# A gate table built from bf16 one-hot rows and three bf16 weight pieces, two tokens at a time

## The chip, the cores and the metric

The kernel runs on one core of a Trainium2 chip. TensorE (PE in the profile) multiplies matrices, and its weight loads have a row of their own (PEld). VectorE (DVE), ScalarE (ACT) and GpSimd (POOL) work on elements, SyncE (SP) issues DMAs. Every number is in microseconds (us) of device time unless it is marked ns, and the metric is the time of one launch.

## The reference, cut to what matters

The reference is one encoder block: two attention branches, an output projection, then a PEER layer with 16,384 experts and a final norm. The change lies in the PEER layer alone:

```python
def block(xb):                       # 128 tokens
    q = (xb @ w_q).reshape(PEER_BLOCK, PEER_HEADS, 2, PEER_HALF)
    ...
    idx = jnp.take_along_axis(cand_i, top_pos, axis=-1)      # i1*128 + i2
    g = jax.nn.softmax(top_s, axis=-1).reshape(PEER_BLOCK, -1)
    h = jnp.einsum('tkd,td->tk', u[idx], xb)
    act = g * jax.nn.gelu(h, approximate=False)
    return jnp.einsum('tk,tkd->td', act, v[idx])
```

Each token uses 8 heads x 16 = 128 experts. An expert has two keys, `i1` and `i2`, each below 128, and a gate weight `g`.

## The kernel before, in words

Everything is in fp32 precision: a matrix product is three fp32r matmuls (helper `mm3`, lines 218 to 221), of a high and a low half of each operand. The halves of a weight tile are made by `wtile`: DMA by SP (L206), high half by ACT (L207), low half by DVE (L208).

Of the 512 tokens, the first 352 (`ND`) are *dense*: the kernel computes all 16,384 experts for them and multiplies each by a gate that is zero where the token did not choose the expert. The other 160 tokens are served by gathered rows (L1115, by POOL; used by DVE at L1126 and L1133). The dense part has two long loops:

- the loop over `e` at L1171 (called the first expert loop here): 128 steps, each of two half steps with 24 matmuls of 128x352; ACT applies gelu (L1192) and stores the result to memory;
- the loop over `i` at L1242 (the second expert loop), which loads gelu results and gates, multiplies them and multiplies by `v`.

The gates come from a table built during the first loop. The generator `gates_of` (L1005) makes it for each of three token tiles (128, 128 and 96 tokens). The keys and gate weights are turned so that the 128 choices of a token lie on the partitions. For one token, the table of 128x128 gates is the product of two one-hot matrices: `oh1[k, i2]` as TensorE's moving or stationary side, and `oh0[k, i1]` scaled by the gate weight. Four tokens go together: DVE compares both keys with 0..127 (L1025, one instruction for 8 rows of 128), ACT scales `oh0` by the high and by the low half of the weight (L1022, eight instructions), and TensorE runs eight fp32r matmuls of 128x128 (L1033), two to each token. `gate_out` (L1040) has ACT copy the bank of four tokens from PSUM (L1053, two instructions), and POOL sends 32 tokens at a time to memory (L1058). One `next(gate_steps)` in each half step (L1186) moves this on; a bank of four tokens takes two half steps. The one-hot rows and their scaled copies lie in unused columns of `hgh` and `hgl` (`spare`, L999).

`routing` (L1063) runs in the same loop, ahead of the gates: the top 16 of the candidates of each token tile, on DVE (L842 to L888). The order of each engine's instructions is made by the framework's scheduler from the order in which the program emits them.

Of the kernel before, what the change touches and what calls it, by code (L numbers as in the profile page):

```python
# [9 lines left out]
F32 = mybir.dt.float32  # L10
F32R = mybir.dt.float32r
BF16 = mybir.dt.bfloat16
# [38 lines left out]
CONST = {}  # L51


def _constants():
# [16 lines left out]
    out, o = [], 0  # L71
    for k, v in cols.items():
        v = np.asarray(v, np.float64).astype(np.float32)
        CONST[k] = (o, o + v.shape[1])
        o += v.shape[1]
        out.append(v)
    return np.ascontiguousarray(np.concatenate(out, axis=1))
# [30 lines left out]
def _layout(x, positions, meta_tokens, norm_mix_g, w_in, mla_q_norm_g, mla_w_uq, mla_kv_norm_g,  # L108
# [50 lines left out]
    for i, n in enumerate(FRONT):  # L159
# [9 lines left out]
            "pos": c(pos[None]), "gains": c(gains), "const": CONST_ARR,  # L169
# [13 lines left out]
def body(tc, nc, a, dbg=None):  # L183
# [55 lines left out]
    cst = cp.tile([P, CONST_ARR.shape[1]], F32, name="cst")  # L239

    def C(k):
        return cst[:, CONST[k][0]:CONST[k][1]]

# [30 lines left out]
    mp = mixer.enter_context(tc.tile_pool(name="mixer", bufs=1, side="left"))  # L274
    tri_r = mp.tile([P, P], F32R, name="tri_r")
# [64 lines left out]
    SP.dma_start(cst, a["const"])  # L340
# [436 lines left out]
    rh_ = hgp.tile([P, SEQ], F32, name="rh_")  # L777
    rcol = hgp.tile([P, 1], F32, name="rcol")
    rcolb = hgp.tile([P, 1], F32, name="rcolb")

    with tc.tile_pool(name="outp", bufs=2, side="right") as op:
# [8 lines left out]
        for m in range(KC):  # L790
# [23 lines left out]
            gr = (op if m < KC - 1 else hgp).tile([P, 2, P], F32, name="gr")  # L814
# [179 lines left out]
    iota_n = up.tile([P, P], F32, name="iota_n", bufs=1)  # L994
    SP.dma_start(iota_n, a["iota"])
    iota_b = iota_n[:, None, None, :].to_broadcast([P, 2, 4, P])
    gb = {}

    spare = [t[:, :, ND:ND + P].rearrange("p (i c t) k -> p i c t k", i=2, c=2) for t in (hgh, hgl)]  # L999
# [5 lines left out]
    def gates_of(ti):  # L1005
        ef, idx = keys[ti], up.tile([P, 2, P], F32, name="idx", bufs=1)
        wt = up.tile([P, 2, P], F32R, name="wt", bufs=1)
# [4 lines left out]
        S.activation(idx, ps[:, :2 * P].rearrange("p (c t) -> p c t", c=2), AF.Copy)  # L1012
# [306 lines left out]
```

## Time and profile before

| | |
|---|---|
| median of three runs | 3683.48 us (3680.32 to 3684.66) |
| the profiled execution | 3683.72 us |
| its span, first to last instruction | 3681.5 us |
| PE busy, share of the span | 3630.1 us, 99% |
| DVE busy | 2623.8 us, 71% |
| ACT busy | 1475.3 us, 40% |
| matmuls of the gate table (L1033) | 704, from 1689.6 to 2509.2 us |

In the rows below a group of instructions is one line of the kernel on one engine, `out<-in` by tile name, `xN` the count, then the busy time, the mean of one in ns, and the idle time ahead of it with what ended it. Matmuls are pipelined, and the end of one is modelled by the profiler; the distance from start to start tells what one costs. The clock column is the granted clock of TensorE as a share of its full 2.4 GHz.

### The profile page before, as it was taken

To read this page: it belongs to the slowest core of one execution; us is meant where nothing else is said; L and a number is where in the kernel's file an instruction comes from. 1 tells how busy PE (TensorE), PEld (TensorE's weight loads), DVE (VectorE), ACT (ScalarE), POOL (GpSimd) and SP (SyncE) were. 2 spreads that over 40 slices of the span, in tenths; PEclk is the share of its full clock that TensorE was granted. 3 is DMA by queue.
4 is the path that set the end of the run, shared out by engine and by line. 5 is a ranking of instruction groups with operands and counts; after the bars stand their busy time and mean duration, and the time that the engine had idled before them with its cause. 6 is when DMAs were issued, how large, how long until landed. Compare 5 with 4: busy or idle time off the path is not lost. (4 is left out here: it accounts for less than half of the span.)

```text
span 3681.5 us, 53353 instructions
## 1 busy us (share of the span) xinstructions
PE 3630.1 (99%) x21159; PEld 3377.5 (92%) x21159; DVE 2623.8 (71%) x3499; ACT 1475.3 (40%) x2360; POOL 702.1 (19%) x499
## 2 busy tenths in 40 slices
PE   9999999999999999999999999999999999999997
PEld 8888888887788878899999999999999999999997
DVE  5533334335644567899979877777689999999896
ACT  4233233234533232235656666664333333333333
POOL 1000000000011221112222322332232322322220
PEclk9999999999999999999999999999999999999998
DMA  4322222221144442268898989999899999999982
GB/s 167 101 100 92 98 93 97 95 98 41 46 143 138 144 156 87 97 250 298 318 351 309 374 335 341 348 342 362 318 374 368 366 365 365 370 357 348 350 335 96
DMA packets 216538, 868.28 MB, mean 236 GB/s; under 512 B 24352, under 2 KB 49632, under 8 KB 175328
## 3 DMA queue, kind: packets, MB, share of 16 engines
q1 hardware_dynamic: 132896, 463.49, 35.4%
q0 software_dynamic: 53440, 361.52, 25.7%
q10 hardware_dynamic: 29952, 39.86, 3.0%
q8 instruction: 166, 2.72, 0.3%
q14 instruction: 84, 0.69, 0.1%
HBM read 801.83 MB, written 62.95 MB: 235 GB/s over the span
## 5 line engine op out<-in xcount | busy, mean ns | idle before, releaser
L207 ACT ACTIVATE wh<-wr 128x1024 fp32r<-128x1024 f32 (+1 forms) x756 | 789.1, 1054 | 1511.5 <-PE ps L221 1346.2
L208 DVE TENSOR_TENSOR wl<-wr,wh 128x1024 fp32r<-128x1024 f32 (+1 forms) x741 | 935.3, 1270 | 512.4 <-ACT wh L207 507.7
L219 PE MATMUL ps<-hgh,wl 128*128 128x352 f32 (+1 forms) x2304 | 773.2, 336 | 10.5 <-DVE wl L208 9.6
L221 PE MATMUL ps<-hgh,wh 128*128 128x352 f32 (+1 forms) x2304 | 768.3, 333 | 0.0
L220 PE MATMUL ps<-hgl,wh 128*128 128x352 f32 (+1 forms) x2304 | 765.1, 332 | 2.1 <-DVE hgl L225 2.0
L219 PE MATMUL ps<-vah,wl 128*128 128x352 f32 x2048 | 664.0, 324 | 4.1 <-DVE wl L208 3.9
L221 PE MATMUL ps<-vah,wh 128*128 128x352 f32 x2048 | 664.8, 325 | 0.0
L220 PE MATMUL ps<-val,wh 128*128 128x352 f32 x2048 | 661.0, 323 | 0.0
L219 PE MATMUL ps<-xh,wl 128*128 128x512 f32 (+1 forms) x1376 | 472.0, 343 | 6.0 <-ACT xh L312 6.0
L220 PE MATMUL ps<-xl,wh 128*128 128x512 f32 (+1 forms) x1376 | 470.1, 342 | 0.2 <-DVE xl L313 0.2
L221 PE MATMUL ps<-xh,wh 128*128 128x512 f32 (+1 forms) x1376 | 470.1, 342 | 0.0
L219 PEld LDWEIGHTS ps<-hgh,wl 128*128 128x128 f32 x2304 | 434.6, 189 | 25.0 <-DVE wl L208 11.9
L220 PEld LDWEIGHTS ps<-hgl,wh 128*128 128x128 f32 x2304 | 434.3, 189 | 14.5 <-DVE hgl L225 2.8
L221 PEld LDWEIGHTS ps<-hgh,wh 128*128 128x128 f32 x2304 | 433.5, 188 | 11.5 <-issue 0.2
L219 PEld LDWEIGHTS ps<-vah,wl 128*128 128x128 f32 x2048 | 386.2, 189 | 5.2 <-DVE wl L208 5.2
L221 PEld LDWEIGHTS ps<-vah,wh 128*128 128x128 f32 x2048 | 388.5, 190 | 0.0
L220 PEld LDWEIGHTS ps<-val,wh 128*128 128x128 f32 x2048 | 388.3, 190 | 0.0
L1115 POOL DMA_INDIRECT row<-v,eo x128 | 217.4, 1698 | 568.4 <-DVE xg L1133 522.7
L1133 DVE SCALAR_TENSOR_TENSOR xg<-row,act,xg 128x2048 f32<-128x2048 f32 x127 | 298.3, 2349 | 7.8 <-DMA row<-v,eo 7.8
L1115 POOL DMA_INDIRECT row<-u,eo x128 | 186.0, 1453 | 610.7 <-DVE row L1126 537.3
L219 PEld LDWEIGHTS ps<-xh,wl 128*128 128x128 f32 x1376 | 259.5, 189 | 37.8 <-ACT xh L312 6.4
L1126 DVE SCALAR_TENSOR_TENSOR row<-row,xg 128x2048 f32<-128x2048 f32 x128 | 292.5, 2285 | 0.5 <-DMA row<-u,eo 0.5
(453 smaller groups left out, 4744.8 us busy)
## 6 DMA issues: line engine op xcount, KB each, us to landing
wr<-ut SPq DMA_DIRECT2D x256, 512.0 KB, 6.3
wr<-vb SPq DMA_DIRECT2D x256, 512.0 KB, 6.7
wr<-front SPq DMA_DIRECT2D x238, 512.0 KB, 3.3
h_d<-hb ACTq DMA_DIRECT2D x128, 176.0 KB, 5.4
g_d<-gb POOLq DMA_DIRECT2D x44, 512.0 KB, 10.5
gin<-g_d SPq DMA_DIRECT2D x32, 704.0 KB, 5.8
hin<-h_d SPq DMA_DIRECT2D x32, 704.0 KB, 7.9
gates<-gt ACTq DMA_DIRECT2D x32, 256.0 KB, 2.0
```

The costliest lines, as they stand in the source:

```text
L207: more["last"] = S.activation(hi[:, s], raw[:, s], AF.Copy)
L208: more["lo"] = (eng or V).tensor_sub(lo[:, s], raw[:, s], hi[:, s].bitcast(F32))
L219: T.matmul(ps, wl, xh, start=start, stop=False)
L220: T.matmul(ps, wh, xl, start=False, stop=False)
L221: T.matmul(ps, wh, xh, start=False, stop=stop)
L1115: G.indirect_dma_start(out=row[:], out_offset=None, in_=a[src], in_offset=bass.IndirectOffsetOnAxis(ap=idx, axis=0))
L1126: ins = V.scalar_tensor_tensor(row, row, 1.0, xg if k < P else xgb, ALU.mult, ALU.mult, accum_out=act[:, k:k + 1] if k < P else actb[:, k ...
L1133: ins = V.scalar_tensor_tensor(y, row, w, y, ALU.mult, ALU.add)
```

## The change

The table is made from bf16 operands. A one-hot row is exact in bf16. The fp32 gate weight is cut into three bf16 pieces (L1029 to L1034 of the changed kernel), which sum to it exactly: DVE makes them by rounding, subtracting, rounding again and subtracting again. A token's table is now three bf16 matmuls, for the three pieces, into the same PSUM columns.

Two tokens go together, and one step of the generator (a half step of the loop) handles one pair: DVE compares the keys of the pair with 0..127 (one instruction, 512 elements of bf16) and multiplies `oh0` by the smallest piece (one instruction, 256 elements); ACT makes the other two scaled copies (four instructions); TensorE runs six matmuls. The two tokens are interleaved in the innermost dimension, so that DVE's operands are contiguous pairs, while TensorE and ACT read every other element. A bank still holds four tokens. There are three buffers of one-hot rows: two in `rh_`, one new tile. `spare` is not used any more. To make room, the constant table is cut in two, one half of which (`MIXER_CONST`) goes when the attention part ends; the 0..127 row is brought into a buffer of the weight ring and turned to bf16 by ACT into `gr_last`.

```diff
-    SP.dma_start(cst, a["const"])
+    SP.dma_start(csts[0], a["const"])
+    SP.dma_start(csts[1], a["const_m"])
...
-    iota_n = up.tile([P, P], F32, name="iota_n", bufs=1)
-    SP.dma_start(iota_n, a["iota"])
-    iota_b = iota_n[:, None, None, :].to_broadcast([P, 2, 4, P])
...
-    spare = [t[:, :, ND:ND + P].rearrange("p (i c t) k -> p i c t k", i=2, c=2) for t in (hgh, hgl)]
+    iota_f = wp.tile([P, 1024], F32, name="wr", tag="wr", bufs=4)[:, :P]
+    SP.dma_start(iota_f, a["iota"])
+    iota_b = gr_last[:, 0].bitcast(BF16).rearrange("p (k t) -> p k t", t=2)
+    S.activation(iota_b, iota_f[:, :, None].to_broadcast([P, P, 2]), AF.Copy)
+    keys_b = gr_last[:, 1].bitcast(BF16).rearrange("p (c t) -> p c t", c=2)
+    more_oh = up.tile([P, 2, P, 2], BF16, name="more_oh", bufs=1)
+    ohs = list(rh_.bitcast(BF16).rearrange("p (i c k t) -> p i c k t", i=2, c=2, t=2)[:, i] for i in range(2)) + [more_oh]
...
-        split(wt[:, 0], wt[:, 1], ps[:, 2 * P:3 * P])
+        w, rest = ps[:, 2 * P:3 * P], ps[:, 3 * P:]
+        V.tensor_copy(last_b, w)
+        V.tensor_copy(wt[:, 0], last_b)
+        V.tensor_sub(rest, w, wt[:, 0])
+        V.tensor_copy(last_b, rest)
+        V.tensor_copy(wt[:, 1], last_b)
+        V.tensor_sub(last_b, rest, wt[:, 1])
         yield
         n = min(P, ND - ti * P)
-        for t0 in range(0, n + 4, 4):
-            if t0:
-                p0 = t0 - 4
-                oh_, wo_ = (spare[c][:, p0 // 4 % 2] for c in range(2))
-                for t in range(4):
-                    for c in range(2):
-                        after_gelu(S.activation(wo_[:, c, t], oh_[:, 0, t].bitcast(F32), AF.Copy,
-                                                scale=wt[:, c, p0 + t:p0 + t + 1].bitcast(F32)))
-            if t0 < n:
-                V.tensor_tensor(spare[0][:, t0 // 4 % 2], idx[:, :, t0:t0 + 4, None].to_broadcast([P, 2, 4, P]),
-                                iota_b, ALU.is_equal)
+        bank = None
+        for p in range(n // 2 + 2):
+            t0 = 2 * p
+            if 0 < p <= n // 2:
+                for t in range(2):
+                    for c in range(2):
+                        after_gelu(S.activation(wos[:, (p - 1) % 2, c, :, t], ohs[(p - 1) % 3][:, 0, :, t], AF.Copy,
+                                                scale=wt[:, c, t0 - 2 + t:t0 - 1 + t]))
+            if p < n // 2:
+                V.tensor_tensor(ohs[p % 3], keys_b[:, :, None, t0:t0 + 2].to_broadcast([P, 2, P, 2]),
+                                iota_b[:, None].to_broadcast([P, 2, P, 2]), ALU.is_equal)
+                V.tensor_tensor(last[:, p % 3], ohs[p % 3][:, 0], last_b[:, None, t0:t0 + 2].to_broadcast([P, P, 2]), ALU.mult)
             yield
             gate_out()
-            if t0:
-                ps = ps_tile()
-                for t in range(4):
-                    for c in range(2):
-                        T.matmul(ps[:, t * P:(t + 1) * P], oh_[:, 1, t], wo_[:, c, t], start=c == 0, stop=c == 1)
-                banks.append((ps, ti * P + p0))
-            yield
+            if p > 1:
+                if p % 2 == 0:
+                    bank = ps_tile()
+                for t in range(2):
+                    o = ((p - 2) % 2 * 2 + t) * P
+                    for c, x in enumerate((last[:, (p - 2) % 3, :, t], wos[:, p % 2, 1, :, t], wos[:, p % 2, 0, :, t])):
+                        T.matmul(bank[:, o:o + P], ohs[(p - 2) % 3][:, 1, :, t], x, start=c == 0, stop=c == 2)
+                if p % 2:
+                    banks.append((bank, ti * P + 2 * (p - 3)))
```

TensorE, in the first expert loop, at the first tokens of the table. Before, eight fp32r matmuls of the table stand between two half steps (L219 to L221 are the experts' matmuls; `hgl` and `hgh` hold the scaled and the plain one-hot rows):

```order
L220 MATMUL ps<-hgl,wh 128x352
L221 MATMUL ps<-hgh,wh 128x352
L1033 MATMUL ps<-hgl,hgh 128x128 x8
L219 MATMUL ps<-hgh,wl 128x352
L220 MATMUL ps<-hgl,wh 128x352
```

In the changed kernel the same place has (L224 to L226 are the experts' matmuls, `rh_` holds the one-hot rows, `last` and `wos` the scaled ones):

```order
L226 MATMUL ps<-hgh,wh 128x352
L1057 LDWEIGHTS rh__9426
L1057 MATMUL ps<-last,rh__9426 128x128
L1057 LDWEIGHTS rh__9426
L1057 MATMUL ps<-wos,rh__9426 128x128
...
L1057 MATMUL ps<-wos,rh__9426 128x128
L224 MATMUL ps<-hgh,wl 128x352
L225 MATMUL ps<-hgl,wh 128x352
```

Six matmuls stand there instead of eight, each with a weight load that is an instruction of its own, and the next six come one half step later, where before there were none until two half steps later.

VectorE, at the start of a token tile's gates, before (L208 is a weight tile's low half, L1126 a gathered row, L845 and L846 the routing, L225 the low half of the gate weights):

```order
L208 TENSOR_TENSOR wl<-wr,wh 128x1024
L845 MAX tv<-wk 128x8
L1126 SCALAR_TENSOR_TENSOR row,act<-row,xg 128x2048
L225 TENSOR_TENSOR wt<-ps,wt 128x128
L1025 TENSOR_TENSOR hgh<-idx,iota_n 128x8x128 x2
L846 MAX_INDEX tp<-tv,wk 128x8
L208 TENSOR_TENSOR wl<-wr,wh 128x1024
```

and now (L213 is the low half, L1150 the gathered row, L1046 the comparison, L1048 the product with the smallest piece):

```order
L1150 SCALAR_TENSOR_TENSOR row,act<-row,xg 128x2048
L1029 CAST last_b<-ps 128x128
L1046 TENSOR_TENSOR rh__9426<-gr_last 128x512
L1030 CAST wt<-last_b 128x128
L1046 TENSOR_TENSOR rh__9426<-gr_last 128x512
L1031 TENSOR_TENSOR ps<-ps,wt 128x128
L1046 TENSOR_TENSOR more_oh<-gr_last 128x512
L1032 CAST last_b<-ps 128x128
L854 MAX_INDEX tp<-tv,wk 128x8
L1033 CAST wt<-last_b 128x128
L213 TENSOR_TENSOR wl<-wr,wh 128x1024
L1034 TENSOR_TENSOR last_b<-ps,wt 128x128
```

Counted from the tile's first own instruction (L225, now L1029), the next weight tile's low half had four instructions ahead of it and now has nine, and in the steps that follow DVE has four instructions for four tokens instead of one.

ScalarE, some steps into the table, before (L207 is a weight tile's high half, L1192 gelu, L1193 its store):

```order
L207 ACTIVATE wh<-wr 128x1024 x2
L1192 ACTIVATE hb<-ps 128x352
L1022 ACTIVATE hgl<-hgh,wt 128x128
L1193 DMA h_d<-hb 128x352
L1022 ACTIVATE hgl<-hgh,wt 128x128 x7
```

and now (L212, L1216 and L1217 are the same three, L1043 the scaled copies):

```order
L212 ACTIVATE wh<-wr 128x1024
L1043 ACTIVATE wos<-more_oh,wt 128x128 x4
L1216 ACTIVATE hb<-ps 128x352
L1043 ACTIVATE wos<-rh__9426,wt 128x128 x4
L1217 DMA h_d<-hb 128x352
L212 ACTIVATE wh<-wr 128x1024 x2
```

The eight scaled copies of four tokens are as many as before, but stand in two fours, one behind the weight tiles of each half step.

## Rows read from the trace of the kernel before

**Rows 1.** The page's busy time of each engine: us, share of the span, instructions.

```profile
PE 3630.1 (99%) x21159; PEld 3377.5 (92%) x21159; DVE 2623.8 (71%) x3499; ACT 1475.3 (40%) x2360; POOL 702.1 (19%) x499
```

**Rows 2.** Stretches of the span from the start of the first expert loop: length, busy time of each engine (with instructions), TensorE's granted clock, share and rate of the DMA engines.

```profile
1600.00:1700.00 100.00, 100.00 (x628) 99.98 (x627) 99.31 (x180) 39.86 (x63) 16.48 (x13) 1.00 0.85 318
1700.00:1800.00 100.00, 92.41 (x571) 89.98 (x571) 99.00 (x160) 63.55 (x139) 24.80 (x19) 0.98 0.81 294
1800.00:1900.00 100.00, 99.44 (x643) 99.30 (x642) 82.94 (x86) 65.99 (x150) 28.76 (x21) 1.00 0.91 346
1900.00:2500.00 600.00, 598.52 (x3860) 598.05 (x3858) 483.56 (x493) 382.57 (x847) 175.98 (x128) 1.00 0.91 341
2500.00:2700.00 200.00, 200.00 (x1246) 200.00 (x1246) 146.36 (x126) 69.57 (x88) 51.74 (x35) 1.00 0.92 352
```

**Rows 3.** Waits in the first expert loop (1590 to 2735 us): engine, tile and line that waited, what it waited for, us in total, times, longest.

```profile
POOL row L1115 <- DVE row L1126: 674.4, 139, 19.6
...
ACT hgl L1022 <- DVE hgh L1025: 60.0, 21, 4.3
...
PE ps L219 <- DVE wl L208: 9.6, 15, 1.8
...
DVE hgh L1025 <- PE ps L1033: 3.5, 6, 0.9
```

**Rows 4.** Groups of instructions, each shape apart, 1370 to 2760 us.

```profile
L219 PE MATMUL ps<-hgh,wl 128*128 128x352 f32 x2048 | 670.8, 328 | 9.6 <-DVE wl L208 9.6
...
L1022 ACT ACTIVATE hgl<-hgh,wt 128x128 fp32r<-128x128 f32 x704 | 219.8, 390 | 65.0 <-DVE hgh L1025 60.0
...
L1025 DVE TENSOR_TENSOR hgh<-idx,iota_n 128x1024 fp32r<-128x1024 f32 x88 | 107.3, 1221 | 4.3 <-PE ps L1033 3.5 <-ACT idx L1012 0.7
...
L1033 PE MATMUL ps<-hgl,hgh 128*128 128x128 f32 x704 | 88.3, 268 | 0.0
...
L225 DVE TENSOR_TENSOR wt<-ps,wt 128x128 fp32r<-128x128 f32 x3 | 0.9, 285 | 0.0
```

**Rows 5.** TensorE's matmuls in order of time around one bank of four tokens: start, length, line.

```profile
2300.44 0.33 PE L220 MATMUL ps<-hgl,wh 128*128 128x352 f32 x1
2300.60 0.33 PE L221 MATMUL ps<-hgh,wh 128*128 128x352 f32 x1
2300.77 1.00 PE L1033 MATMUL ps<-hgl,hgh 128*128 128x128 f32 x8
2301.61 0.38 PE L219 MATMUL ps<-hgh,wl 128*128 128x352 f32 x1
2301.82 0.33 PE L220 MATMUL ps<-hgl,wh 128*128 128x352 f32 x1
```

**Rows 6.** All engines in order of time around a bf16 matmul that stands alone among fp32r ones, in the attention part: start, length, engine and line. PEld is the weight load.

```profile
184.63 0.35 PE L439 MATMUL ps<-qh,kh 128*128 128x400 f32 x1
184.64 0.19 PEld L436 LDWEIGHTS ps<-qh,kl 128*128 128x128 f32 x1
...
184.82 0.29 PE L436 MATMUL ps<-qh,kl 128*128 128x272 f32 x1
184.94 0.10 PEld L437 LDWEIGHTS <-bf 128*128 128x128 bf16 x1
184.94 0.23 PE L437 MATMUL ps<-bf 128*128 128x128 bf16 x1
184.95 0.20 PEld L438 LDWEIGHTS ps<-ql,kh 128*128 128x128 f32 x1
184.98 0.37 PE L438 MATMUL ps<-ql,kh 128*128 128x272 f32 x1
185.07 0.19 PEld L439 LDWEIGHTS ps<-qh,kh 128*128 128x128 f32 x1
185.19 0.29 PE L439 MATMUL ps<-qh,kh 128*128 128x272 f32 x1
...
185.32 0.23 PE L436 MATMUL ps<-qh,kl 128*128 128x144 f32 x1
```

**Rows 7.** All instructions of that bf16 matmul's line in the span: count, then least, median and greatest length in ns, first and last start.

```profile
L437 PEld LDWEIGHTS <-bf x40: 95/96/98, 183.6 to 763.2; 128*128 128x128 bf16 x40
L437 PE MATMUL ps<-bf x40: 183/230/233, 183.6 to 763.2; 128*128 128x128 bf16 x24, 128*128 128x112 bf16 x8, 128*128 128x16 bf16 x8
```

**Rows 8.** Groups of VectorE, each shape apart, over the whole span.

```profile
L884 DVE TENSOR_TENSOR oh<-pf,cst 128x512 f32<-128x512 f32 x32 | 22.1, 690 | 0.7
...
L208 DVE TENSOR_TENSOR wl<-wr,wh 128x256 fp32r<-128x256 f32 x4 | 1.7, 422 | 5.9 <-ACT wh L207 4.4 <-DMA raw<-xt 1.5
...
L509 DVE TENSOR_SCALAR ang<-ang 128x512 f32<-128x512 f32 x1 | 0.4, 427 | 0.0
...
L344 DVE CAST bf<-cst 128x128 bf16<-128x128 f32 x1 | 0.2, 223 | 0.0
```

**Rows 9.** The comparisons of line L1025 between 1600 and 1825 us: count, lengths in ns, first and last start.

```profile
L1025 DVE TENSOR_TENSOR hgh<-idx,iota_n x16: 1212/1219/1222, 1680.8 to 1819.6; 128x1024 fp32r<-128x1024 f32 x16
```

More of the change, by code (lines that the diff above doesn't have):

```diff
@@ L51 @@
 CONST = {}
+MIXER_CONST = ("tri", "perm", "neg", "qlo", "negrow", "freq", "sign", "halfpi")
 def _constants():
@@ L70, in _constants @@
     }
[L71 to L77, printed above, removed]
+    out = []
+    for part in range(2):
+        arrs, o = [], 0
+        for k, v in cols.items():
+            if (k in MIXER_CONST) == bool(part):
+                v = np.asarray(v, np.float64).astype(np.float32)
+                CONST[k] = (part, o, o + v.shape[1])
+                o += v.shape[1]
+                arrs.append(v)
+        out.append(np.ascontiguousarray(np.concatenate(arrs, axis=1)))
+    return out
 CONST_ARR = _constants()
@@ L168, in _layout @@
     return {"front": front, "ut": c(ut), "vb": c(vb), "u": c(u), "v": c(v), "xt": c(xt),
-            "pos": c(pos[None]), "gains": c(gains), "const": CONST_ARR,
+            "pos": c(pos[None]), "gains": c(gains), "const": CONST_ARR[0], "const_m": CONST_ARR[1],
             "iota": c(np.broadcast_to(np.arange(P, dtype=np.float32), (P, P)))}
@@ L238, in body @@
     SP.dma_start(gn, a["gains"])
-    cst = cp.tile([P, CONST_ARR.shape[1]], F32, name="cst")
+    csts = [cp.tile([P, CONST_ARR[0].shape[1]], F32, name="cst")]
     def C(k):
-        return cst[:, CONST[k][0]:CONST[k][1]]
+        return csts[CONST[k][0]][:, CONST[k][1]:CONST[k][2]]
     def gain(k):
@@ L274, in body @@
     mp = mixer.enter_context(tc.tile_pool(name="mixer", bufs=1, side="left"))
+    csts.append(mp.tile([P, CONST_ARR[1].shape[1]], F32, name="cst_m"))
     tri_r = mp.tile([P, P], F32R, name="tri_r")
@@ L777, in body @@
     rh_ = hgp.tile([P, SEQ], F32, name="rh_")
+    gr_last = hgp.tile([P, 2, P], F32, name="gr_last")
     rcol = hgp.tile([P, 1], F32, name="rcol")
@@ L813, in body @@
                     G.tensor_add(rh_, rh_, sq)
-            gr = (op if m < KC - 1 else hgp).tile([P, 2, P], F32, name="gr")
+            gr = op.tile([P, 2, P], F32, name="gr") if m < KC - 1 else gr_last
             V.tensor_scalar(gr[:, 0], xr[:, TA:], gm, None, ALU.mult)
@@ L990, in body @@
     up = stage.enter_context(tc.tile_pool(name="up", bufs=2, side="left"))
-    iota_n = up.tile([P, P], F32, name="iota_n", bufs=1)
-    SP.dma_start(iota_n, a["iota"])
-    iota_b = iota_n[:, None, None, :].to_broadcast([P, 2, 4, P])
     gb = {}
-    spare = [t[:, :, ND:ND + P].rearrange("p (i c t) k -> p i c t k", i=2, c=2) for t in (hgh, hgl)]
+    iota_f = wp.tile([P, 1024], F32, name="wr", tag="wr", bufs=4)[:, :P]
[5 more added lines that the diff above has]
+    ohs = list(rh_.bitcast(BF16).rearrange("p (i c k t) -> p i c k t", i=2, c=2, t=2)[:, i] for i in range(2)) + [more_oh]
+    wos = up.tile([P, 2, 2, P, 2], BF16, name="wos", bufs=1)
+    last = up.tile([P, 3, P, 2], BF16, name="last", bufs=1)
+    last_b = up.tile([P, P], BF16, name="last_b", bufs=1)
+    wt = up.tile([P, 2, P], F32, name="wt", bufs=1)
     def after_gelu(ins):
@@ L1005, in gates_of @@
     def gates_of(ti):
-        ef, idx = keys[ti], up.tile([P, 2, P], F32, name="idx", bufs=1)
-        wt = up.tile([P, 2, P], F32R, name="wt", bufs=1)
+        ef = keys[ti]
         ps = ps_tile()
@@ L1011, in gates_of @@
             T.transpose(ps[:, j * P:(j + 1) * P], src, ident)
-        S.activation(idx, ps[:, :2 * P].rearrange("p (c t) -> p c t", c=2), AF.Copy)
-        split(wt[:, 0], wt[:, 1], ps[:, 2 * P:3 * P])
+        S.activation(keys_b, ps[:, :2 * P].rearrange("p (c t) -> p c t", c=2), AF.Copy)
+        w, rest = ps[:, 2 * P:3 * P], ps[:, 3 * P:]
[4 more added lines that the diff above has]
+        V.tensor_copy(wt[:, 1], last_b)
```

## The prediction

> **What bounds the kernel now.** I read the busy times first: TensorE is busy for 99% of the span, VectorE for 71%, ScalarE for 40% [rows 1]. A busy TensorE need not be at its peak, so I looked next at the stretches [rows 2]. From 1900 to 2700 us it hardly pauses (1.5 us), at a granted clock of 1.00 (the 2.4 GHz level), while in the first 600 us of it VectorE has 116 us idle, ScalarE 217 us, and the DMA engines stand at 0.91. There, what TensorE has to do sets the time, one for one. From 1600 to 1800 us it is different: VectorE is busy for 99%, and between 1700 and 1800 us TensorE loses 7.6 us of 100. The waits say to whom [rows 3]: TensorE waited 9.6 us in 15 pieces for VectorE's low half of a weight tile (L208), and next to nothing else. That is the stretch in which routing, gathered rows, weight halves and the first gates all want VectorE. So an instruction of the gate table is paid on TensorE everywhere, on VectorE only up to about 1825 us, and on ScalarE nowhere unless it makes a weight half late. After the table's last matmul nothing is changed, and all of it moves with the end of the first loop.
>
> **TensorE: what is removed.** Line L1033 is 704 fp32r matmuls of 128x128 [rows 4]. Their 268 ns each is a modelled length and no price. The price is in the order of time [rows 5]: L221 at 2300.60, eight of the table, L220 at 2301.82, which is 1.22 us for two steps of the experts' matmuls and the eight. A step is 200 us / 1246 = 0.160 us where there is no table, from 2500 to 2700 us [rows 2]. So eight cost 1.22 - 0.32 = 0.90 us, 0.112 us each, and the 88 banks 79.2 us.
>
> **TensorE: what is added.** 1056 bf16 matmuls of 128x128 with a load each, in 176 groups of six. Before has no two bf16 matmuls in a row; it has 40 that stand alone among fp32r ones [rows 7]. One is shown [rows 6]: from the 272-column matmul L436 at 184.82 to the next group's L436 at 185.32 are 0.50 us, for three fp32r matmuls of 272 columns (0.124 us each by the 0.160 us for 352 columns, 0.37 together) and the bf16 one: it costs 0.13 us. Where this goes: its load starts at 184.94, just when the 272 columns are through, though the fp32r loads start under the matmul before (L436's at 184.64, one hundredth after L439's matmul began). The next fp32r load follows at 184.95 and the one behind it at 185.07, 0.12 later. So the 0.13 us are about 0.02 for the bf16 load, which nothing hides, and 0.11 for the fp32r load behind it, under whose cover the bf16 columns pass. In a group of six the five first have a bf16 load behind them instead: I take 0.058 us for 128 columns (0.160 x 128/352) plus the 0.02 of an unhidden load, 0.078; the last costs 0.13. That is 5 x 0.078 + 0.13 = 0.52 us for a group and 176 x 0.52 = 91.5 us, 12.3 us more than before. Bounds: with all loads hidden six are 6 x 0.058 = 0.35 us (61.6 us in all, 17.6 less than before); if each costs what the lone one costs, 0.78 us (137.3 us, 58.1 more). I take the middle value because in the 40 rows the load waits for the columns but is itself short (0.10 us in the record against 0.19 of an fp32r one, whose step is 0.11 to 0.12).
>
> The TensorE page of the Trainium skill ("TensorE: Matmul & The Clock Gate", Step-by-step) says otherwise: TensorE pulls a weight load ahead of matmuls in flight, so that the next tile's weights load while this one streams. The row shows that this did not happen between an fp32r matmul and a bf16 load; no row shows two of bf16. By that rule a step is the 0.058 of the first rival below.
>
> Of the 12.3 us, what falls into the stalls of 1720 to 1800 us is hidden by TensorE's wait: nine experts with two groups of 0.07 us extra, 1.3 us.
>
> **VectorE.** A comparison of four tokens is 1221 ns, 88 times [rows 4]. Now two pairs take two comparisons of 512 bf16 elements and two products of 256. A two-tensor instruction of 512 fp32 elements is 690 ns and one of 256 is 422 ns; one of a tensor and a constant, of 512, is 427 ns [rows 8]: the engine has a double rate for some forms. If bf16 operands get it, a comparison is like 256 elements, 0.42 us, and a product like the 128 of L225, 0.285 us [rows 4]: 1.41 us for four tokens, 0.19 more. If not, 2 x (0.69 + 0.42) = 2.22, 1.0 more. Below, with four elements at a time, 2 x (0.285 + 0.22) = 1.01, 0.2 less. I take 1.41: the pairs are contiguous and have half the bytes, as a row of double rate would need.
>
> The page "VectorE: DVE Perf Modes" (The perf-mode tier table) has two-tensor instructions on bf16 at twice the rate of fp32 and never at four times. No row of before has such an instruction. By it the value taken holds and the lower end falls away.
>
> Where it counts: 16 comparisons lie between 1680 and 1820 us [rows 9], in the stretch where VectorE is the limit; 16 x 0.19 = 3.1 us. The cutting of the weights is six small instructions instead of one: four casts of about 0.22 us [rows 8] and two subtractions of 0.285, 1.45 - 0.29 = 1.2 us, once in that stretch. Together 4.3 us, taken as wait of TensorE one for one (queued behind them are the L208 halves that TensorE waits for). The other 72 banks, 14 us, and two cuttings fall into VectorE's idle time after 1825 us (116 us of 600); without that cover they would cost the 14 us.
>
> **ScalarE, DMA, the rest.** The scaled copies stay 704 of 390 ns [rows 4] and stand at 64% of ScalarE's time. They follow their comparison by one half step instead of two. ScalarE waited 60.0 us in 21 pieces for comparisons [rows 3] with two; while it waits, the high halves of weight tiles queue behind it, and L208 behind these. I cost this at nothing: it waits most where VectorE is full anyway, and VectorE then works on what is ahead of the weight halves. The cover ends where VectorE is not full; then each wait of up to 4.3 us could pass on, a few us in all. VectorE's own 3.5 us of waiting for the table's matmuls goes, with a third buffer; it was in slack. The table of 0..127 takes one place in the ring of four weight buffers at the start of the loop, and one ScalarE instruction: TensorE is busy 100 of 100 us behind it [rows 2], so nothing, at most about 2 us. Two DMAs of constants for one, and three moved small casts, lie under the first matmuls: nothing. POOL's table stores keep their number and place.
>
> **Sum.** Against the profiled execution's 3683.7 us (median 3683.5): 3683.7 + 12.3 - 1.3 + 4.3 = 3699.0 us.
>
> **Rivals.**
>
> *bf16 loads hide among themselves.* Only the step into fp32r is paid: 5 x 0.058 + 0.13 = 0.42 us, 73.9 us in all, 5.3 less than before; with VectorE's 4.3 us 3682.7. For: fp32r loads do start under the matmul before. Against: the 40 bf16 loads did not. The Trainium skill's rule of loads pulled ahead gives this case.
>
> *TensorE gains all of it.* All loads hide, the one back into fp32r too: 61.6 us, 17.6 less, with 4.3 for VectorE 3670.4. Against: the lone row pays 0.11 for that last load.
>
> *bf16 gets no double rate on VectorE.* Place: 1680 to 1820 us. 16 x 1.0 + 1.2 = 17.2 us of wait for L208 instead of 4.3, with TensorE as forecast 3711.9. It decides from the point where VectorE has no idle time, which rows 2 show up to 1825 us. For: interleaved and broadcast operands. Against: the pairs are contiguous.
>
> *Every bf16 matmul pays like the lone one* (load and columns one after the other, each with a full latency): 58.1 + 4.3, 3746. Against: most of the lone price is an fp32r load that is not there inside a group.
>
> **How the numbers follow.** About 0.2% (7.4 us, so 3676.1 to 3690.9 is no change) is what a measurement of this kernel can tell. Chances: forecast 0.37, loads hidden among themselves 0.27, all hidden 0.13, no double rate 0.15, lone price 0.08. Faster: the 0.13 and the lower edge of the hidden-load case, 0.05 (if VectorE costs nothing), 0.18. No change: the rest of that case, 0.22, and 0.04 of the forecast's lower edge, 0.26. Slower: 0.56. The range leaves out one in ten on each side: below, most of the case of 3670; above, the case of 3746 and a little: 3672 to 3730. As the cases lie on both sides, the forecast's own range is 3690 to 3708 (a bf16 load of 0.01 to 0.03 us).
>
> **What would show it.** In the changed kernel's order of time: the distance from the last expert matmul before a group to the second one behind it, less 0.32, should be 0.52 us; 0.42 is the first rival, 0.35 the second, 0.78 the last. The bf16 loads of a group should start about 0.078 us apart. The comparison should be 0.42 us long and the product 0.29; 0.69 and 0.42 is the third rival. TensorE's loss between 1700 and 1800 us should rise from 7.6 to about 11 us, and the second expert loop should be as long as before. I am wrong if the groups cost what I say and the end does not move with them, or if ScalarE's waits for comparisons reach TensorE.

## The result, and the profile after

The changed kernel takes 3657.45 us (median of four runs, 3653.41 to 3664.64), the kernel before 3684.07 us beside it (four runs, 3680.32 to 3685.76). The ratio is 0.9931, 95% interval [0.9913, 0.9949]: 26.6 us less, between 19 and 32. The forecast was 3699 us with a range of 3672 to 3730, so both the size and the sign were wrong. The profiled execution took 3664.64 us (span 3662.9 us), the longest of the four; by it the gain is 19.1 us. Two later comparisons of the same two kernels, described below, gave 20.6 and 18.0 us by their medians, so 26.6 is at the upper end of what the change is worth.

The page's busy time of each engine, to be read against [rows 1]:

```profile
PE 3619.2 (99%) x21511; PEld 3346.0 (91%) x21511; DVE 2628.3 (72%) x3778; ACT 1477.9 (40%) x2358; POOL 671.1 (18%) x499
```

TensorE has 352 matmuls more and is busy 11 us less; VectorE has 279 instructions more and is busy 4.5 us more. So the added work is there, but TensorE does not pay for it as forecast. The stretches, as in [rows 2]:

```profile
1600.00:1700.00 100.00, 100.00 (x632) 99.59 (x631) 98.09 (x187) 39.80 (x59) 16.77 (x13) 1.00 0.84 317
1700.00:1800.00 100.00, 100.00 (x700) 97.00 (x699) 99.31 (x185) 68.58 (x153) 25.27 (x20) 1.00 0.87 325
1800.00:1900.00 100.00, 100.00 (x697) 97.14 (x696) 91.24 (x139) 65.27 (x143) 26.59 (x22) 1.00 0.96 363
1900.00:2000.00 100.00, 100.00 (x674) 97.91 (x673) 93.30 (x157) 57.34 (x121) 25.50 (x20) 1.00 0.93 346
2000.00:2500.00 500.00, 500.00 (x3489) 485.43 (x3487) 400.33 (x544) 333.79 (x739) 132.93 (x113) 1.00 0.92 344
2500.00:2700.00 200.00, 200.00 (x1243) 200.00 (x1242) 147.24 (x125) 66.54 (x75) 45.22 (x31) 1.00 0.93 357
```

Between 1700 and 1800 us VectorE is as full as before (99.31), but TensorE, which lost 7.6 us there, loses nothing and issues 700 matmuls in place of 571. From 1800 to 1900 us VectorE is now at 91 where it was at 83: work has moved to there. The waits from 1590 to 2735 us (engine, tile and line that waited, what for, us in total, times, longest), against [rows 3]:

```profile
POOL row L1139 <- DVE row L1150: 499.6, 102, 20.1
...
ACT wos L1043 <- DVE rh__9426 L1046: 25.5, 16, 2.9
...
DVE rh__9426 L1046 <- PE ps L1057: 13.9, 13, 2.6
...
ACT wos L1043 <- DVE more_oh L1046: 11.4, 7, 3.9
DVE more_oh L1046 <- PE ps L1057: 8.0, 8, 2.7
...
PEld ps L224 <- DVE wl L213: 5.2, 2, 2.7
...
PE ps L224 <- DVE wl L213: 4.6, 2, 2.4
```

None of TensorE's 15 waits for weight halves is left in the first loop: the two that remain stand at 2723 and 2729 us, where the second loop has begun (in before the like of them, 3.9 us, stands at 2745 us, behind the window's end). ScalarE waits less for comparisons (36.9 us in 23 pieces; it was 60.0 in 21). VectorE now waits 21.9 us for the table's matmuls, where it waited 3.5; as TensorE waits for nothing in the first loop, that costs nothing.

TensorE and its weight loads in order of time around one group of six (start, length, engine, line), to be read against [rows 5]:

```profile
2303.24 0.32 PE L226 MATMUL ps<-hgh,wh 128*128 128x352 f32 x1
2303.40 0.35 PEld L1057 LDWEIGHTS <-rh__9426 128*128 128x128 bf16 x6
2303.41 0.23 PE L1057 MATMUL ps<-last,rh__9426 128*128 128x128 bf16 x1
2303.48 0.28 PE L1057 MATMUL ps<-wos,rh__9426 128*128 128x128 bf16 x2
2303.60 0.22 PE L1057 MATMUL ps<-last,rh__9426 128*128 128x128 bf16 x1
...
2303.66 0.28 PE L1057 MATMUL ps<-wos,rh__9426 128*128 128x128 bf16 x2
2303.71 0.19 PEld L224 LDWEIGHTS ps<-hgh,wl 128*128 128x128 f32 x1
2303.74 0.41 PE L224 MATMUL ps<-hgh,wl 128*128 128x352 f32 x1
2303.82 0.19 PEld L225 LDWEIGHTS ps<-hgl,wh 128*128 128x128 f32 x1
2303.98 0.32 PE L225 MATMUL ps<-hgl,wh 128*128 128x352 f32 x1
```

From L226 at 2303.24 to L225 at 2303.98 are 0.74 us for two steps of the experts and the six; less 0.32 they cost 0.42. The median over all 176 groups is the same, taken to the nanosecond from the trace's starts: 740 - 2 x 160.5 = 419 ns, or 73.7 us in all. For the eight fp32r matmuls of before, the same working gives 896 ns, or 78.8 us. So the table is 5.1 us cheaper on TensorE. Inside a group the starts are 71, 59, 58, 58 and 57 ns apart (medians), and 58 ns is what 128 columns take at the experts' rate (0.160 us x 128/352): the bf16 loads cost nothing there. From the second on, a load starts within 11 ns of the start of the matmul ahead of it. What is left, 0.419 - 6 x 0.058 = 0.071 us, lies at the borders. The last bf16 matmul and L224 start almost together (26 ns apart in the middle value), and L225 then comes 246 ns behind L224, not 160. The starts say where the 0.071 us go. The first bf16 load waits until the columns of L226 are through (2303.40), which costs some 18 ns. The other 53 lie behind the last bf16 matmul: from L224's load to L225's are 108 ns (median), much like the 112 ns between the fp32r loads of the table in before, and only the 58 ns of columns of that matmul cover it.

The new instructions of VectorE and ScalarE (count, least/median/greatest ns, first and last start), in three answers by line. The comparison:

```profile
L1046 DVE TENSOR_TENSOR rh__9426<-gr_last x118: 406/420/468, 1681.1 to 2479.8; 128x512 bf16<-128x512 bf16 x118
```

The product with the smallest piece:

```profile
L1048 DVE TENSOR_TENSOR last<-rh__9426,last_b x118: 266/286/294, 1686.7 to 2480.2; 128x256 bf16<-128x256 bf16 x118
```

The scaled copies:

```profile
L1043 ACT ACTIVATE wos<-rh__9426,wt x472: 414/428/458, 1681.6 to 2485.5; 128x128 bf16<-128x128 bf16 x158
```

The comparison is 0.42 us and the product 0.286, as forecast, so four tokens cost VectorE 1.41 us against 1.22. The page "VectorE: DVE Perf Modes" of the Trainium skill (The perf-mode tier table) has two-tensor instructions on bf16 at twice the rate of fp32, and the row agrees: 512 elements in 420 ns against 690 in fp32 [rows 8], near the 422 of half as many. ScalarE's copies are a tenth longer (428 against 390 ns).

**Where in the run the time went.** The whole time scatters by some 10 us from run to run, which hides a part of 5 us. The trace gives a sharper measure: the starts of the 12,288 matmuls of 352 columns, counted in order of time. The first 6,144 are the first expert loop (to about 2656 us in before, so the waits above take in the second loop's first 80 us or so); nothing of the change lies behind it. In us, from the start of one matmul to that of another, for all the kernels of this study (the experiments are described below):

| kernel | #0 to #1024 | to #1280 | to #1536 | to #6143 | first loop | second loop |
|---|---|---|---|---|---|---|
| before | 174.7 | 55.1 | 46.7 | 810.9 | 1087.4 | 1005.8 |
| changed | 172.5 | 45.9 | 45.8 | 803.5 | 1067.7 | 1008.0 |
| changed_again | 172.4 | 45.9 | 45.8 | 803.5 | 1067.6 | 1005.0 |
| changed_third | 173.3 | 45.9 | 45.8 | 803.5 | 1068.5 | 998.8 |
| before_routing_later | 171.9 | 46.7 | 45.9 | 809.0 | 1073.5 | 1002.8 |
| after_routing_later | 172.4 | 45.9 | 45.8 | 803.5 | 1067.6 | 1004.1 |
| twelve_matmuls | 174.9 | 50.0 | 50.0 | 853.4 | 1128.2 | 1000.1 |
| singles | 175.4 | 49.3 | 49.5 | 854.1 | 1128.4 | 998.7 |
| two_pieces | 171.2 | 44.6 | 44.5 | 787.1 | 1047.4 | 1007.9 |
| pairs_together | 171.4 | 45.5 | 48.2 | 799.6 | 1064.7 | 1011.5 |
| pairs_routing_later | 172.3 | 45.2 | 46.0 | 799.6 | 1063.1 | 1005.5 |

Three executions of the changed kernel agree within 0.9 us in the first loop; the second loop differs by up to 13 us between executions of code that is the same there. The change is worth 19.7 us in the first loop. 9.2 of these fall into 256 matmuls, about 1744 to 1799 us, and 7.4 are spread over the rest of the table.

The 9.2 are not all waits. In before eleven matmuls in that stretch, from 1788.9 to 1792.2 us, start 293 ns apart in place of 160: behind the longest wait of TensorE (1.8 us) the granted clock is at its lower level, 1.2 GHz, which costs 1.5 us.

```profile
1790.00:1800.00 10.00, 10.00 (x60) 10.00 (x59) 9.96 (x19) 7.46 (x16) 2.83 (x2) 0.89 0.73 274
```

The changed kernel has eleven such matmuls too, but at the start of the loop (granted clock 0.83 from 1565 to 1575 us, where before has 1.00), so the totals of the two can be compared. All other traces have ten to sixteen there, except those of twelve_matmuls and pairs_together, which have none: their first loops are 1.5 us shorter by that alone.

What VectorE did while TensorE ran the matmuls #768 to #1280 gives a reason, which the experiments below test. Groups of VectorE in that stretch, of before (1694.5 to 1799 us), the three largest of routing:

```profile
L886 DVE TENSOR_TENSOR oh<-oh,i1f 128x512 f32<-128x512 f32 x8 | 5.5, 692 | 0.1
L888 DVE TENSOR_REDUCE ef<-oh 128x32 f32<-128x512 f32 x8 | 5.5, 685 | 0.1
L884 DVE TENSOR_TENSOR oh<-pf,cst 128x512 f32<-128x512 f32 x7 | 4.8, 692 | 0.2
```

The same of the changed kernel (1695 to 1786.5 us, the same 512 matmuls):

```profile
L892 DVE TENSOR_TENSOR oh<-pf,cst 128x512 f32<-128x512 f32 x6 | 4.2, 705 | 0.1
L894 DVE TENSOR_TENSOR oh<-oh,i1f 128x512 f32<-128x512 f32 x6 | 4.2, 694 | 0.1
L896 DVE TENSOR_REDUCE ef<-oh 128x32 f32<-128x512 f32 x6 | 4.1, 680 | 0.1
```

Each of routing's large instructions is there seven or eight times before and six times now. All lines of routing (L842 to L901 before) add up to 37.6 us there, and to 26.5 us in the changed kernel: 11 us of routing are done at another time. The gathered rows are as many (15, 34.3 us), and of weight halves there are 22 before and 21 now. The order of VectorE's queue says the same. Routing's instructions that stand ahead of the n-th weight half, counted from the end of the router's scores:

| weight half | 24 | 30 | 36 | 42 | 48 | 54 | 60 | 66 |
|---|---|---|---|---|---|---|---|---|
| before | 162 | 182 | 206 | 228 | 251 | 273 | 273 | 273 |
| changed | 162 | 175 | 198 | 211 | 223 | 246 | 260 | 273 |
| before_routing_later | 162 | 182 | 185 | 204 | 207 | 212 | 229 | 229 |

In the changed kernel the scheduler has put routing instructions of the second token tile behind weight halves that they stood ahead of: 28 of them at the 48th. VectorE is full in both kernels; what differs is what TensorE gets out of it first.

### The profile page after: what moved, and what is told of

Read it like the earlier page. It is cut to its first block, busy times and chain, and to the rows that moved or that the text cites. A ratio compares the mean times of both kernels' runs of the same rounds, so it can differ in the third digit from the quotient of the medians.

```text
span 3662.9 us, 54428 instructions
## 1 busy us (share of the span) xinstructions
PE 3619.2 (99%) x21511; PEld 3346.0 (91%) x21511; DVE 2628.3 (72%) x3778; ACT 1477.9 (40%) x2358; POOL 671.1 (18%) x499
## 4 chain that ended last, share of the span: by engine, by line
PE 91%; DVE 4%; DMA 2%; issue 2%; ACT 1%; SPq 0%; DVEq 0%; ACTq 0%
PE ps L224 29%; PE ps L226 28%; PE ps L225 28%; PE ps L1057 2%; DVE xg L1157 1%; DVE wl L213 1%; DMA wr<-vb 1%; DMA hin<-h_d 1%; DVE acc L1315 1%; PE ps L703 0%; DVE val L230 0%; PE ps L712 0%; ACT wh L212 0%; PE ps L445 0%; DVE acc L1260 0%
## 5 line engine op out<-in xcount | busy, mean ns | idle before, releaser
L212 ACT ACTIVATE wh<-wr 128x1024 fp32r<-128x1024 f32 (+1 forms) x756 | 795.4, 1056 | 1574.6 <-PE ps L226 1424.7
L213 DVE TENSOR_TENSOR wl<-wr,wh 128x1024 fp32r<-128x1024 f32 (+1 forms) x741 | 936.0, 1269 | 469.7 <-ACT wh L212 466.3
L224 PE MATMUL ps<-hgh,wl 128*128 128x352 f32 (+1 forms) x2304 | 780.9, 339 | 0.8 <-ACT hgh L229 0.8
L226 PE MATMUL ps<-hgh,wh 128*128 128x352 f32 (+1 forms) x2304 | 767.2, 333 | 0.0
L225 PE MATMUL ps<-hgl,wh 128*128 128x352 f32 (+1 forms) x2304 | 764.1, 332 | 2.1 <-DVE hgl L230 2.0
L224 PE MATMUL ps<-vah,wl 128*128 128x352 f32 x2048 | 663.5, 324 | 5.9 <-DVE wl L213 5.7
L226 PE MATMUL ps<-vah,wh 128*128 128x352 f32 x2048 | 663.4, 324 | 0.0
L225 PE MATMUL ps<-val,wh 128*128 128x352 f32 x2048 | 659.6, 322 | 0.0
L224 PE MATMUL ps<-xh,wl 128*128 128x512 f32 (+1 forms) x1376 | 471.1, 343 | 5.9 <-ACT xh L318 5.9
L225 PE MATMUL ps<-xl,wh 128*128 128x512 f32 (+1 forms) x1376 | 469.3, 341 | 0.2 <-DVE xl L319 0.2
L226 PE MATMUL ps<-xh,wh 128*128 128x512 f32 (+1 forms) x1376 | 469.1, 341 | 0.0
L225 PEld LDWEIGHTS ps<-hgl,wh 128*128 128x128 f32 x2304 | 434.2, 188 | 14.3 <-DVE hgl L230 2.8
L224 PEld LDWEIGHTS ps<-hgh,wl 128*128 128x128 f32 x2304 | 433.9, 188 | 12.5 <-ACT hgh L229 1.3
L226 PEld LDWEIGHTS ps<-hgh,wh 128*128 128x128 f32 x2304 | 433.0, 188 | 11.5 <-issue 0.2
L224 PEld LDWEIGHTS ps<-vah,wl 128*128 128x128 f32 x2048 | 385.3, 188 | 7.5 <-DVE wl L213 7.5
L226 PEld LDWEIGHTS ps<-vah,wh 128*128 128x128 f32 x2048 | 388.1, 189 | 0.0
L225 PEld LDWEIGHTS ps<-val,wh 128*128 128x128 f32 x2048 | 387.4, 189 | 0.0
L224 PEld LDWEIGHTS ps<-xh,wl 128*128 128x128 f32 x1376 | 259.1, 188 | 37.9 <-ACT xh L318 6.4
L1150 DVE SCALAR_TENSOR_TENSOR row<-row,xg 128x2048 f32<-128x2048 f32 x128 | 292.3, 2283 | 1.9 <-DMA row<-u,eo 1.9
L225 PEld LDWEIGHTS ps<-xl,wh 128*128 128x128 f32 x1376 | 259.6, 189 | 33.1 <-DVE xl L319 1.3
```

The source lines that it names most:

```text
L212: more["last"] = S.activation(hi[:, s], raw[:, s], AF.Copy)
L213: more["lo"] = (eng or V).tensor_sub(lo[:, s], raw[:, s], hi[:, s].bitcast(F32))
L224: T.matmul(ps, wl, xh, start=start, stop=False)
L225: T.matmul(ps, wh, xl, start=False, stop=False)
L226: T.matmul(ps, wh, xh, start=False, stop=stop)
L1150: ins = V.scalar_tensor_tensor(row, row, 1.0, xg if k < P else xgb, ALU.mult, ALU.mult, accum_out=act[:, k:k + 1] if k < P else actb[:, k ...
```

## The experiments

Three theories stand after the result. A: most of the gain comes from routing's new place in VectorE's queue, and the cheaper table on TensorE gives some 5 us. B: TensorE's loss in before came from the table's own work on VectorE and ScalarE, which the change made finer. C: TensorE's matmuls give all of it.

**Routing's place alone, in the kernel before and in the changed one.** The first step of routing for each two heads of token tiles 0 and 1 is put behind the weight half that was emitted last; the order alone, no wait on another engine. `before_routing_later` is the kernel before with these lines:

```diff
-            V.tensor_tensor(cand, vv[:, :, 0, :, None].to_broadcast(shp), vv[:, :, 1, None, :].to_broadcast(shp), ALU.add)
+            c_ = V.tensor_tensor(cand, vv[:, :, 0, :, None].to_broadcast(shp), vv[:, :, 1, None, :].to_broadcast(shp), ALU.add)
+            if ti in (0, 1):
+                tc.add_manual_dep(c_.ins, more["lo"].ins.name, NOSYNC, reason="not before its step's weights")
```

> The kernel before, fp32r table and all; only the first comparison-free step of routing (the sum of candidates, one in nine steps) of the token tiles 0 and 1 may not stand ahead of the weight half of its own step in VectorE's queue. Theory A (the loss of 13 us between 1695 and 1799 us was routing of the next token tile, placed too early in VectorE's queue; the change pushed it back): TensorE no longer loses 7.6 us in 1700 to 1800 us, the launch is 10 to 14 us shorter than before, 3670 to 3674. Theory B (the loss came from the table's own work, the 1.2 us comparisons and the eight scaled copies in a row that hold up the high halves): the loss stays, 3680 to 3686. Theory C (all 26 us come from TensorE's matmuls): no change.

`after_routing_later` is the changed kernel with the same lines:

> The changed kernel with the same rule for routing. Theory A: the routing is out of the way already, so within 3 us of the changed kernel (3655 to 3661), and 4 to 8 us under the kernel before with the same rule, which is TensorE's part alone (176 x 0.419 against 88 x 0.896 us, 5.1 us less). Theory B: also the same as the changed kernel, but 17 us or more under the kernel before with that rule. Theory C: as B.

`changed_again` is the changed kernel as it is:

> The changed kernel beside the other two on the same chip: 3653 to 3665, 20 to 30 us under the kernel before.

Measured beside the kernel before at 3678.80 us (eight runs): before_routing_later 3663.15 us (ratio 0.9964, [0.995, 0.9978]), after_routing_later 3660.04 (0.9947, [0.9928, 0.9966]), changed_again 3658.17 (0.9941, [0.9924, 0.9957]). The first is 15.6 us under before, a little more than the 10 to 14 expected; the second is only 3.1 us under the first, where 4 to 8 were expected, but both scatter by 9 to 11 us. The stretches of before_routing_later:

```profile
1700.00:1800.00 100.00, 100.00 (x650) 100.00 (x649) 90.53 (x114) 69.40 (x157) 29.37 (x21) 1.00 0.91 346
1800.00:1900.00 100.00, 100.00 (x646) 100.00 (x645) 91.78 (x113) 61.53 (x130) 30.90 (x21) 1.00 0.91 343
```

Three lines in the old kernel, with every fp32r matmul of the table left in place, take TensorE's loss between 1700 and 1800 us away, and VectorE is no longer full there. Of the 20.6 us between before and changed in this comparison, 15.6 come with routing's place; in the first loop 13.9 of 19.7. B and C fall. In the changed kernel the same lines bring nothing: its first loop is 1067.6 us with and without them. And between the two kernels with routing moved, where only the table differs, there are 5.9 us of first loop; the groups' price says 5.1. TensorE waits for nothing in the first loop of either.

**What a matmul inside a group costs.** `twelve_matmuls` has each of the six twice, so that the table's values are doubled:

```diff
-                    for c, x in enumerate((last[:, (p - 2) % 3, :, t], wos[:, p % 2, 1, :, t], wos[:, p % 2, 0, :, t])):
+                    for c, x in enumerate((last[:, (p - 2) % 3, :, t], last[:, (p - 2) % 3, :, t], wos[:, p % 2, 1, :, t], wos[:, p % 2, 1, :, t], wos[:, p % 2, 0, :, t], wos[:, p % 2, 0, :, t])):
...
```

> The changed kernel with each matmul of the table done twice in a row, so that the table is twice what it should be; the operands and all else stay. If bf16 loads hide among themselves (0.058 us for each added matmul): 176 x 6 x 0.058 = 61 us more than the changed kernel, about 3718. With the 0.078 us of the prediction's sum: 82 us more, 3740. If TensorE does not set the end in the first loop: less than 50 us.

`two_pieces` leaves out the smallest piece, its product on VectorE and a third of the matmuls:

```diff
-                V.tensor_tensor(last[:, p % 3], ohs[p % 3][:, 0], last_b[:, None, t0:t0 + 2].to_broadcast([P, P, 2]), ALU.mult)
...
-                    for c, x in enumerate((last[:, (p - 2) % 3, :, t], wos[:, p % 2, 1, :, t], wos[:, p % 2, 0, :, t])):
+                    for c, x in enumerate((wos[:, p % 2, 1, :, t], wos[:, p % 2, 0, :, t])):
...
```

> The changed kernel without the smallest piece of the gate weights: four matmuls in a group instead of six, and no product on VectorE. If TensorE alone sets the time there: 176 x 2 x 0.058 = 20.4 us less than the changed kernel, about 3637. If VectorE's 176 products of 0.286 us (50 us) also cost: more than 25 us less.

`singles` takes the groups apart: one matmul of the table behind each of the first six sets of three expert matmuls of a half step. It changes the table's values, since operands are overwritten before they are read.

```diff
-                        T.matmul(bank[:, o:o + P], ohs[(p - 2) % 3][:, 1, :, t], x, start=c == 0, stop=c == 2)
+                        spread.append((bank[:, o:o + P], ohs[(p - 2) % 3][:, 1, :, t], x, c))
...
+                if spread:
+                    o_, w_, x_, c_ = spread.pop(0)
+                    T.matmul(o_, w_, x_, start=c_ == 0, stop=c_ == 2)
...
```

> The changed kernel with the six matmuls of a group spread out, one behind each of the first six sets of three expert matmuls of the next half step. If what a bf16 matmul costs is set by its neighbours (0.13 us alone among fp32r ones, 0.058 inside a group): 6 x 0.13 = 0.78 us instead of 0.42, 176 x 0.36 = 63 us more than the changed kernel, about 3720. If grouping does not matter: no change.

One execution of each gave 3714.86, 3643.3 and 3714.94 us (the kernel before 3684.11). The first loops are sharper: twelve_matmuls 60.5 us longer than changed (62.0 with the 1.5 us of the clock), where 176 x 6 x 0.058 = 61.2 was expected; two_pieces 20.3 us shorter, where 176 x 2 x 0.058 = 20.4 was. So a further bf16 matmul in a group costs its columns and no more, and VectorE's 176 products, which two_pieces leaves out, cost nothing. The group of twelve in order of time:

```profile
2303.51 0.33 PE L226 MATMUL ps<-hgh,wh 128*128 128x352 f32 x1
2303.68 0.29 PE L1057 MATMUL ps<-last,rh__9426 128*128 128x128 bf16 x2
2303.81 0.39 PE L1057 MATMUL ps<-wos,rh__9426 128*128 128x128 bf16 x4
2304.04 0.28 PE L1057 MATMUL ps<-last,rh__9426 128*128 128x128 bf16 x2
2304.16 0.39 PE L1057 MATMUL ps<-wos,rh__9426 128*128 128x128 bf16 x4
2304.36 0.41 PE L224 MATMUL ps<-hgh,wl 128*128 128x352 f32 x1
2304.60 0.32 PE L225 MATMUL ps<-hgl,wh 128*128 128x352 f32 x1
```

It takes 1.09 - 0.32 = 0.77 us, 0.35 more than six. The single one:

```profile
2300.14 0.32 PE L226 MATMUL ps<-hgh,wh 128*128 128x352 f32 x1
2300.30 0.10 PEld L1214 LDWEIGHTS <-more_oh 128*128 128x128 bf16 x1
2300.31 0.23 PE L1214 MATMUL ps<-last,more_oh 128*128 128x128 bf16 x1
2300.31 0.20 PEld L224 LDWEIGHTS ps<-hgh,wl 128*128 128x128 f32 x1
2300.35 0.41 PE L224 MATMUL ps<-hgh,wl 128*128 128x352 f32 x1
2300.43 0.19 PEld L225 LDWEIGHTS ps<-hgl,wh 128*128 128x128 f32 x1
2300.59 0.32 PE L225 MATMUL ps<-hgl,wh 128*128 128x352 f32 x1
```

From L226 to L225 are 0.45 us, less 0.32 are 0.13: the price read in [rows 6] is right for a matmul that stands alone, and 1056 of them make the first loop 60.7 us longer (1056 x 0.13 - 73.7 = 63.6 expected). Its load starts where the 352 columns are through, and both fp32r loads behind it come 0.12 us apart. The loss of 0.07 us is one for each way into bf16 and back, not one for each bf16 load: it is 0.073 for a single matmul, 0.074 for the groups of four in two_pieces, 0.071 for six, 0.071 for the twelve here.

**Fewer borders.** If a group costs 0.071 us at its borders, two groups in a row cost that once. `pairs_together` emits the matmuls of two pairs together, with a buffer more of each operand; `changed_third` is the changed kernel beside it.

```diff
...
-            if p > 1:
-                if p % 2 == 0:
-                    bank = ps_tile()
+            if p > 1 and p % 2:
+                bank = ps_tile()
+                for q in (p - 3, p - 2):
+                    for t in range(2):
...
+                banks.append((bank, ti * P + 2 * (p - 3)))
...
```

> The changed kernel with the matmuls of two neighbouring groups emitted together: 88 chains of twelve in place of 176 of six, with a fourth buffer for the one-hots and the smallest piece and a third for the scaled rows. Nothing else changes: the same matmuls, comparisons, products and copies. Theory (a group costs six steps of 0.058 us plus 0.071 us for going into bf16 and out again): a chain of twelve costs 0.77 us where two of six cost 0.84, so 88 x 0.071 = 6.3 us less, some 3651 us where the changed kernel has 3657. Rival (the 0.071 us belongs to each group's own first matmul and its operands, or TensorE waits at these places anyway): no difference, within 2 us. Second rival (fewer and longer chains come later, and what waits for the gate table is late): slower than the changed kernel.

> The changed kernel once more, as the measure for the run beside it: 3654 to 3662 us, ratio to the kernel before 0.993 to 0.994.

Measured 3657.97 us (ratio 0.9939, [0.9924, 0.9953]) against 3658.48 for changed_third (0.9944, [0.993, 0.9958]): no difference in the whole time. A chain of twelve costs 0.770 us (median, 1091 - 2 x 160.5 ns), as expected, which saves 88 x (0.838 - 0.770) = 6.0 us on TensorE. The first loop is only 3.0 us shorter than that of changed, and 1.5 of these are the clock at its start. The table shows where most of the rest is: 2.4 us more between #1280 and #1536. The waits say on what (TensorE's own, 1590 to 2735 us):

```profile
PE ps L224 <- DVE wl L213: 7.2, 5, 2.4
```

Three of the five waits for weight halves lie in the first loop, at 1723, 1792 and 1819 us, where changed has none; they make the distances there 2.9 us longer. (The other two are at the start of the second loop, as in changed.) TensorE, now faster, has caught up with VectorE. That leaves some 1.6 us of the 6.0 unaccounted for. `pairs_routing_later` adds the order of before_routing_later to it:

> Chains of twelve as in pairs_together, and the routing of tiles 0 and 1 put behind the weight halves as in after_routing_later. Theory (pairs_together gained 5.7 us in its chains and gave some 2.5 of it back in waits for weight halves between 1700 and 1850 us): the waits go, and the first loop, from its first matmul to its 6,656th, takes some 1,144 us, where the changed kernel takes 1,149.8 and pairs_together 1,146.8; of the whole time it is 3 us less than pairs_together, if the second loop's own scatter of some 10 us lets that be seen: 3,652 to 3,656. Rival (the chains of twelve themselves delay the copies and comparisons that wait for them): the loop stays at 1,147.

Measured 3648.78 us (3643.66 to 3658.55, five runs), ratio 0.9922, [0.9909, 0.9936], to the kernel before: 29.8 us less, the lowest median of the kernels that ran more than once, and below the 3652 to 3656 expected. The first loop is 1063.1 us, 4.6 less than that of changed. To the 6,656th matmul, as the expectation counts, it is 1145.1 us, near the 1144 of the theory and not the 1147 of the rival. The wait between #1280 and #1536 goes (46.0 in place of 48.2), and of TensorE's waits one is left, at 2723 us in the second loop. Of the chains' 6.0 us 4.6 arrive; where the rest goes is open.

```profile
PE ps L224 <- DVE wl L213: 2.3, 1, 2.3
```

Its stretch of 1700 to 1800 us:

```profile
1700.00:1800.00 100.00, 100.00 (x707) 98.43 (x706) 89.18 (x144) 68.72 (x157) 26.24 (x20) 1.00 0.91 334
```

The interval overlaps those of the changed kernel, whose ratios were 0.9931, 0.9941 and 0.9944. That it is faster by its 4.6 us rests on the first loop, not on the whole time.

## Why the prediction was wrong

- **What bounds the kernel** was read rightly: TensorE, and from 1700 to 1800 us VectorE's low halves ahead of it. The step from there, that an instruction of the table on VectorE is paid in that stretch one for one, took the rest of VectorE's queue as fixed. It was not.
- **TensorE, what is removed:** 79.2 us forecast, 78.8 measured.
- **TensorE, what is added:** 91.5 us forecast, 73.7 measured. The step that failed is "0.058 us for 128 columns (0.160 x 128/352) plus the 0.02 of an unhidden load, 0.078" for the five bf16 matmuls that have a bf16 load behind them. The 0.02 is right for the change from fp32r to bf16, which is all that [rows 6] show, and is not there between two bf16 matmuls: 0.058 (twelve_matmuls and two_pieces, within 2%). The 0.13 of the last one was right (0.419 - 5 x 0.058 = 0.129). With that the term is -5.1 us in place of +12.3. The first rival had exactly this group, 0.42 us. The rule weighed there, that TensorE pulls weight loads ahead of matmuls in flight ("TensorE: Matmul & The Clock Gate" of the Trainium skill, Step-by-step), holds in this trace among bf16 matmuls (the loads of a group from the second on, 11 ns or less behind the start of the matmul ahead), and not at the border from fp32r, where the bf16 load still starts with the end of the columns (2300.30 above).
- **The 1.3 us hidden in the stalls** had no stall left to hide in.
- **VectorE:** 0.42, 0.285 and 1.41 us were right to 2 ns, so the rival without double rate falls. The step that failed is the 4.3 us "taken as wait of TensorE one for one". TensorE's loss from 1700 to 1800 us, which was to rise from 7.6 to about 11 us, went to 0, and two_pieces shows that the products cost it nothing. Routing was never priced: the prediction took the order of all that the diff does not touch as given. The larger part of the effect lay there: 13.9 us of first loop, as before_routing_later shows. (16 x 0.19 is 3.0, not 3.1, a slip without weight.)
- **ScalarE and the rest:** at nothing, as forecast; the copies' extra 38 ns stayed in slack. So did VectorE's waiting for the table's matmuls, though it did not go, as forecast, but rose from 3.5 to 21.9 us. The second loop is as long as before but for its scatter.

Summed again with the measured terms: 3683.7 - 5.1 (table) - 13.9 (routing's place, as measured in the kernel before) = 3664.7. The two failed steps make up the 34.3 us between this and the forecast: 17.4 by the bf16 matmuls, 18.2 by VectorE's queue, less the 1.3 that were to be hidden. The profiled execution has 3664.6. So close a match is luck: its first loop is 19.7 us shorter than that of before, not 19.0, the part ahead of the loop 1.0 shorter, and the second loop 2.2 longer. The second rival's 3670 would have been near by number; its mechanism, all loads hidden, is not what happened, for the way into bf16 and back is still paid.

Open is why the scheduler put routing later: the comparison is cut in two and stands with other instructions around it, but no run changed that alone. The products are not the reason: in two_pieces, which has none, 250 routing instructions stand ahead of the 54th weight half, against 246 in changed and 273 in before. The place in before_routing_later is also not the same as in the changed kernel (the table of weight halves); it shows that routing's place is worth 14 us, not that exactly this place was taken.

## What to carry to other kernels

Where an engine is full, look in its queue at what stands ahead of the instructions that the bottleneck waits for, before and after, and not only at what the edit adds: an edit can reorder work that it does not touch, and here that was worth more than twice the edit itself. A price read from an instruction that stands alone among others of another type is the price of going there and back; before it is multiplied by a count, ask how many such borders there are. Where the whole time scatters, the distance between two matmuls of the same number in both traces measures a stage to within 1 us, once stretches at the lower clock are counted.

## What was not expected of the hardware

The step of the experts' matmuls is not one number. In the second loop, with the same instructions, TensorE busy for the whole stretch and a granted clock of 1.00, the changed kernel's trace has two rates:

```profile
2840.00:2940.00 100.00, 100.00 (x623) 100.00 (x622) 92.06 (x87) 30.95 (x30) 30.35 (x17) 1.00 0.95 357
...
3240.00:3340.00 100.00, 100.00 (x627) 100.00 (x626) 92.96 (x84) 31.43 (x29) 26.66 (x16) 1.00 0.96 364
```

And that of changed_third a third one:

```profile
2940.00:3040.00 100.00, 100.00 (x632) 100.00 (x631) 91.67 (x84) 32.59 (x30) 30.58 (x17) 1.00 0.96 368
```

That is 161.1, 160.0 and 158.9 ns for 352 columns (from start to start, the mean over each stretch), each held for hundreds of us, and at other places in each execution. Over 6,144 matmuls, 2.2 ns are 14 us, about as much as the second loop's scatter (998.7 to 1011.5 us). It is not all of it: in the longest second loop, that of pairs_together, TensorE is busy for only 98.03 us from 3040 to 3140 us and 97.71 from 3340 to 3440, with a granted clock of 0.98 in both. The granted clock does not show the three rates, and their cause was not tried.
